# The RWKV-7 scan of a two-layer kernel without block-diagonal tiles

## The chip, the cores and the metric

The kernel runs on one core of a Trainium2 chip, as one program. The metric is the device time of one execution in microseconds (us). The time before is the median of 3 runs. The engines are named as in the profile: PE is TensorE's matrix products and PEld its weight loads, DVE is VectorE, ACT is ScalarE, POOL is GpSimd, SP is SyncE, which issues most of the DMAs.

## The reference

The program computes a hybrid block of two layers at width 1024 over 256 context and 1024 latent tokens, 1280 in all. The even layer mixes tokens by an mLSTM and an RWKV-7 head group, the odd one by HGRN2 and a latent attention. Each layer has a modulation and an MLP. The change concerns one piece of the even layer, the RWKV-7 recurrence, with 8 heads of 64 channels and two directions (the second runs over the flipped tokens):

```python
def rwkv7_scan(r, w, k, v, a_vec, b_vec):
    Z, T, H, dk = k.shape
    dv = v.shape[-1]
    xs = tuple(jnp.moveaxis(t, 1, 0) for t in (r, w, k, v, a_vec, b_vec))

    def step(S, inp):
        rt, wt, kt, vt, at, bt = inp
        sa = jnp.einsum('zhvk,zhk->zhv', S, at)
        S = S * wt[:, :, None, :] + sa[..., None] * bt[:, :, None, :] + vt[..., None] * kt[:, :, None, :]
        return S, jnp.einsum('zhvk,zhk->zhv', S, rt)

    _, y = lax.scan(step, jnp.zeros((Z, H, dv, dk), jnp.float32), xs)
    return jnp.moveaxis(y, 0, 1)
...
    y = rwkv7_scan(z(r), z(decay[0], decay[1]), z(key_d[0], key_d[1]), z(v), z(-kk), z(icl[0], icl[1]))
    y = head_groupnorm(dir_merge(y, B, n_ctx), rw_ln_w, rw_ln_b) + bonus
```

For each token the state S (64x64 a head) is decayed by w, corrected by the product of S with a and b, and given the outer product of v and k. The output is S times r. The two directions are added and normalized by head.

## The kernel before

**Tiling.** Tokens lie in 10 tiles of 128 (NT). The scan is computed in chunks of 64 tokens, two (cc) in a tile, so a direction has 20 chunk visits and both have 40. Within a chunk the recurrence is a triangular system: with u for the vector of all S·a of the chunk, u is the inverse of a triangular 64x64 matrix times a right-hand side that depends on the state at the chunk's start. The stage before (its products L854 to L936 are seen in rows of the prediction) computes these inverses, one for each head and chunk, and writes them to DRAM (xcd). Heads come in four pairs f; head e of a pair (0 or 1) lies on partitions 64e to 64e+63.

**The scan stage.** scan(d), L1001 to L1143, is a Python generator for direction d. L1278 weaves four generators with each other, a piece of each in turn: the gates of the mLSTM, scan(1), scan(0) and, at a rate of 0.6, the modulation's products (L245, with weights adaw that stream from HBM by DMA on SP's queue). From this order, and from priorities, a scheduler of the framework makes the order of instructions on each engine when the kernel is built; each engine then works through its own list and waits on semaphores. In this stage PSUM's eight banks are tagged (L986): three "ch" for the products of the ring, three "am" for the products that prepare a tile, one "mo" for the modulation, and one "ps" that only the gates use, at the start.

For each tile, load (L1004) issues the DMAs on SP's queue:

- CM holds the factors a and r with decay worked in, BK those of b and k (both from DRAM, by the stage before).
- ZV holds, for each chunk and head of a pair, the state on one partition half and v on the other. Later u takes the place of the state.
- XB[d][i], two buffers for each direction, holds the inverses of the pairs as block-diagonal 128x128 matrices. The off-diagonal blocks are set to zero once (L996, L997), and two DMAs a tile, one for each partition half, put the 64x64 inverses into the diagonal blocks (L1017).

amat (L1022) then prepares the tile in three parts: the products of BK with CM for each chunk (L1034), masked by VectorE into CM (L1037) and copied by ScalarE into AM (L1040 to L1042) for GpSimd to mask (L1044), and the turned BK (L1046 to L1056), which ScalarE copies into KB. These parts are done a tile ahead, between the chunk visits.

**One chunk visit** goes as follows (4 pairs f, the two heads e of a pair as two products each):

1. L1086, L1087: right-hand side pr, from CM and ZV (128 rows by 64 columns). L1089: VectorE copies it to rs.
2. L1094: pu = inverse times rs. The stationary operand is a column half of the block-diagonal XB, so 128 rows are read, of which 64 are zeros. Both heads go into one bank, on two partition halves. L1096: VectorE copies rows 0 to 63 of u into ZV; L1097: ScalarE copies rows 64 to 127.
3. L1105, L1106: pz, from KB and ZV. L1108: VectorE adds the state Zc to give t1. L1111, L1112: VectorE multiplies t1 by the chunk's decay (wlast) into ZV of the next chunk, half by half. L1114: GpSimd makes the next Zc from the same. L1116, L1117: ScalarE copies the new state from ZV into the block-diagonal ZB[d][i], whose other blocks are zeros (L996, L997, and L1070).
4. L1125, L1127: the output py. For each f come first two products of ZB (a column half, 128 rows) with r in CM, then two of u and v in ZV with AM, added to the same place in PSUM. L1134: ScalarE copies the output to yt, in the direction that reaches a tile first; in the other VectorE adds the first one's output, loaded back from DRAM (L1137).

A chunk's ring is 1, 2 and 3: the next right-hand side needs the state of L1111 and L1112. Step 4 is needed by nothing in the ring but stands in TensorE's list. After the second direction has done a tile, finish (L1145 to L1165) normalizes it and writes it out. The mLSTM stage follows, from about 1081 us of the span.

Of the kernel before, what the change touches and what calls it, by code (L numbers as in the profile page):

```python
# [17 lines left out]
P = 128  # L18
# [137 lines left out]
def _body(tc, nc, I, out, dbg, stop, es):  # L156
# [827 lines left out]
    with ExitStack() as ph:  # L984
# [6 lines left out]
        yfd = dram([NT, P, 4, P], "yfd")  # L991
        hfd = dram([NT, P, 512], "hfd")

        XB = [[rp.tile([P, 2, 4, P], F32, name=f"XB{d}{i}") for i in range(2)] for d in range(2)]
        ZB = [[rp.tile([P, 4, P], F32, name=f"ZB{d}{i}") for i in range(2)] for d in range(2)]
        for t_ in XB[0] + XB[1] + ZB[0] + ZB[1]:  # L996
            G.memset(t_, 0.0)  # L997
        lnb_eps = rp.tile([P, 1], F32, name="lneps")
        V.memset(lnb_eps, RW_GN_EPS)

        def scan(d):  # L1001
            bst4 = strict.unsqueeze(1).to_broadcast((P, 4, 64))

            def load(step):  # L1004
                c = ORD[d][step]
                xb = XB[d][step % 2]
                CM = rp.tile([P, 4, 3, P], F32, tag="CM", name=nm("CM"), bufs=4)
                BK = rp.tile([P, 4, 2, 2, 64], F32, tag="BK", name=nm("BK"), bufs=3)
                ZV = rp.tile([P, 2, 2, 4, 64], F32, tag="ZV", name=nm("ZV"), bufs=4)
                SY.dma_start(CM[0:64, :, 0:2, :], ard[d][c, 0:64])  # L1010
                SY.dma_start(CM[64:128, :, 1:3, :], ard[d][c, 64:128])
                SY.dma_start(BK, bkd[d][c])
                for e in range(2):
                    q = slice(64 * e, 64 * e + 64)
                    SY.dma_start(ZV[64 - 64 * e:128 - 64 * e, :, e].rearrange("p c f v -> p c (f v)"),
                                 vtd[d][c * P:(c + 1) * P, e].rearrange("(c t) f v -> t c (f v)", c=2))
                    SY.dma_start(xb[q, :, :, 64 * e:64 * e + 64].rearrange("p c f t -> p (c f) t"),  # L1017
                                 xcd[d, q, 2 * c:2 * c + 2].rearrange("p c f t -> p (c f) t"))
                return dict(c=c, xb=xb, CM=CM, BK=BK, ZV=ZV)

            def amat(o):
# [38 lines left out]
            for part in amat(cur):  # L1060
                part()
                yield
            zi = 0
            for cc_ in (0,):
                G.memset(cur["ZV"][0:64, 0, 0], 0.0)
                G.memset(cur["ZV"][64:128, 0, 1], 0.0)
            Zc = rp.tile([P, 4, 64], F32, tag=f"Zc{d}", name=nm("Zc"), bufs=2)
            G.memset(Zc, 0.0)
            for i in range(2):
                G.memset(ZB[d][i], 0.0)  # L1070
            for step in range(NT):
                nxt, parts = None, []
                if step + 1 < NT:
# [5 lines left out]
                for cc in range(2):  # L1079
                    tk = slice(64 * cc, 64 * cc + 64)  # L1080
                    last = step == NT - 1 and cc == 1
                    uv, zb = ZV[:, cc], ZB[d][zi % 2]
                    pr = ps(256, tag="ch")
                    for f in range(4):
                        o = pr[:, f * 64:f * 64 + 64]
# [2 lines left out]
                    rs = rp.tile([P, 4, 64], F32, tag="rs", name=nm("rs"), bufs=2)  # L1088
                    V.tensor_copy(rs, pr.rearrange("p (f v) -> p f v", f=4))  # L1089
                    yield  # L1090
                    pu = ps(256, tag="ch")
                    for f in range(4):
                        for e in (0, 64):
                            TE.matmul(pu[e:e + 64, f * 64:f * 64 + 64], xb[:, cc, f, e:e + 64], rs[:, f, :], start=True, stop=True)  # L1094
                    puv = pu.rearrange("p (f v) -> p f v", f=4)
                    V.tensor_copy(uv[0:64, 0], puv[0:64])  # L1096
                    S.copy(uv[64:128, 1], puv[64:128])  # L1097
                    if parts:
                        parts.pop(0)()
                    yield  # L1100
                    if not last:
                        pz = ps(256, tag="ch")
                        for f in range(4):
                            o = pz[:, f * 64:f * 64 + 64]
                            TE.matmul(o[0:64], KB[:, 0, cc, f, :], uv[:, 0, f, :], start=True, stop=True)  # L1105
                            TE.matmul(o[64:128], KB[:, 1, cc, f, :], uv[:, 1, f, :], start=True, stop=True)  # L1106
                        t1 = rp.tile([P, 4, 64], F32, tag="t1", name=nm("t1"), bufs=2)
                        V.tensor_tensor(t1, pz.rearrange("p (f v) -> p f v", f=4), Zc, op=ALU.add)  # L1108
                        wb = wlast[:, d, :, 2 * c + (cc if d == 0 else 1 - cc)].unsqueeze(2).to_broadcast((P, 4, 64))
                        zn = ZV[:, 1] if cc == 0 else nxt["ZV"][:, 0]  # L1110
                        V.tensor_tensor(zn[0:64, 0], t1[0:64], wb[0:64], op=ALU.mult)  # L1111
                        V.tensor_tensor(zn[64:128, 1], t1[64:128], wb[64:128], op=ALU.mult)  # L1112
                        Zc = rp.tile([P, 4, 64], F32, tag=f"Zc{d}", name=nm("Zc"), bufs=2)
                        G.tensor_tensor(Zc, t1, wb, op=ALU.mult)  # L1114
                        zbn = ZB[d][(zi + 1) % 2]
                        S.copy(zbn[0:64, :, 0:64], zn[0:64, 0])  # L1116
                        S.copy(zbn[64:128, :, 64:128], zn[64:128, 1])  # L1117
                    if parts and cc:
                        parts.pop(0)()
                    yield  # L1120
# [1 line left out]
                    for f in range(4):  # L1122
                        o = py[:, f * 64:f * 64 + 64]
                        for e in (0, 64):
                            TE.matmul(o[e:e + 64], zb[:, f, e:e + 64], CM[:, f, 1, tk], start=True, stop=False)  # L1125
                        for e in range(2):
                            TE.matmul(o[64 * e:64 * e + 64], uv[:, e, f, :], AM[:, cc, e, f, :], start=False, stop=True)  # L1127
                    zi += 1
                    pyv = py.rearrange("p (f t) -> p f t", f=4)
                    if cc == 0 and not first:  # L1130
                        yo = rp.tile([P, 4, P], F32, tag=f"yo{d}", name=nm("yo"), bufs=1)
# [885 lines left out]
```

## Time and profile before

| | |
|---|---|
| time, median of 3 runs | 4004.09 us (3995.06 to 4010.38) |
| the profiled execution's own time | 3995.29 us |
| its span, first to last instruction | 3993.5 us |
| TensorE's granted clock over the span (1 is full speed) | 0.952 |
| the stage before the scan, its last 50 us (715 to 765 us): TensorE busy, clock | 39.3 us, 0.85 |
| the scan stage (765 to 1081 us): its length | 316 us |
| the mLSTM stage, its first 79 us (1081 to 1160 us): TensorE busy, clock | 57.6 us, 0.87 |
| the scan's output products, L1125 and L1127: TensorE busy | 44.9 and 44.6 us |
| the u products, L1094 | 29.8 us |

The profile is of one execution, and its own time stands 9 us below the median of the runs. In the rows of the profile, a group such as "L1125 PE MATMUL ps<-CM,ZB 128*64 128x64 f32 x640" names the line, the engine, the operation, the tile written and those read, and the tile form: "128*64" means that 128 rows and 64 columns of the array are used; "128x64" is the moving operand, and x640 the count. Two products whose forms leave room for each other (two column halves, or two row halves) run side by side. Behind the shape stand the busy time in us and the mean duration of one in ns, then the idle time of the engine before them and what ended it. "<-issue" means that nothing that the profile shows was waited for. A row of a timeline has the start in us from the span's start, the length, the engine and the group; [0.47 <-X] is idle time ahead of it that X ended.

### The profile page before, as it was taken

To read this page: it belongs to the slowest core of one execution; us is meant where nothing else is said; L and a number is where in the kernel's file an instruction comes from. 1 tells how busy PE (TensorE), PEld (TensorE's weight loads), DVE (VectorE), ACT (ScalarE), POOL (GpSimd) and SP (SyncE) were. 2 spreads that over 40 slices of the span, in tenths; PEclk is the share of its full clock that TensorE was granted. 3 is DMA by queue.
4 is the path that set the end of the run, shared out by engine and by line. 5 is a ranking of instruction groups with operands and counts; after the bars stand their busy time and mean duration, and the time that the engine had idled before them with its cause. 6 is when DMAs were issued, how large, how long until landed. Compare 5 with 4: busy or idle time off the path is not lost. (4 is left out here: it accounts for less than half of the span.)

```text
span 3993.5 us, 67013 instructions
## 1 busy us (share of the span) xinstructions
PE 3634.5 (91%) x26934; PEld 3113.5 (78%) x26934; DVE 2308.7 (58%) x3891; ACT 1346.4 (34%) x2569; POOL 1493.1 (37%) x1532
## 2 busy tenths in 40 slices
PE   5999989888788799999999989988888979999998
PEld 3888879766577698998999878976666758888887
DVE  5565553355557656556656632338878466666655
ACT  3444342354533432214222232223344434223221
POOL 3044646433333443324332221334444535333332
PEclk7999999899889899999999999989999989999999
DMA  4454646779577632223222276222122364334332
GB/s 168 124 135 126 164 117 160 190 215 230 178 259 260 202 91 86 80 75 116 80 80 69 83 223 194 92 100 73 59 81 72 108 198 127 100 101 137 95 100 74
DMA packets 534911, 521.33 MB, mean 131 GB/s; under 512 B 128296, under 2 KB 443624, under 8 KB 534600
## 3 DMA queue, kind: packets, MB, share of 16 engines
q1 hardware_dynamic: 438904, 441.03, 37.7%
q10 hardware_dynamic: 82080, 35.17, 3.1%
q0 software_dynamic: 13616, 40.84, 2.9%
q8 instruction: 212, 3.47, 0.4%
q14 instruction: 99, 0.81, 0.1%
HBM read 395.79 MB, written 121.16 MB: 129 GB/s over the span
## 5 line engine op out<-in xcount | busy, mean ns | idle before, releaser
L281 ACT CAST wh<-raw 128x1024 fp32r<-128x1024 f32 x330 | 341.2, 1050 | 1000.5 <-PE ps L288 502.1
L286 PE MATMUL ps<-mh,wh 128*128 128x384 f32 (+2 forms) x1888 | 630.5, 334 | 4.5 <-ACT mh L337 3.0
L288 PE MATMUL ps<-mh,wl 128*128 128x256 f32 (+2 forms) x1888 | 626.8, 332 | 4.4 <-POOL wl L282 4.4
L287 PE MATMUL ps<-mh,wh 128*128 128x256 f32 (+2 forms) x1888 | 626.8, 332 | 0.0
L471 DVE TENSOR_TENSOR relu<-relu 128x384 f32<-128x384 f32 (+1 forms) x192 | 332.7, 1733 | 396.7 <-ACT relu L470 396.6
L282 POOL TENSOR_TENSOR wl<-raw,wh 128x1024 fp32r<-128x1024 f32 x145 | 351.6, 2425 | 538.7 <-ACT wh L281 537.1
L286 PE MATMUL ps<-wh,h1h 128*128 128x512 f32 x1152 | 450.5, 391 | 5.1 <-ACT acc L502 2.7
L287 PE MATMUL ps<-wl,h1h 128*128 128x512 f32 x1152 | 449.3, 390 | 0.0
L288 PE MATMUL ps<-wh,h1l 128*128 128x512 f32 x1152 | 449.3, 390 | 0.0
L504 DVE TENSOR_TENSOR acc<-ps,acc 128x512 f32<-128x512 f32 x540 | 359.2, 684 | 153.3 <-PE ps L288 150.7
L473 POOL TENSOR_TENSOR h1l<-relu,h1h 128x384 fp32r<-128x384 f32 (+1 forms) x192 | 202.5, 1055 | 531.6 <-DVE h1h L472 527.4
L286 PEld LDWEIGHTS ps<-mh,wh 128*128 128x128 f32 x1888 | 357.8, 190 | 38.9 <-issue 11.1
L288 PEld LDWEIGHTS ps<-mh,wl 128*128 128x128 f32 x1888 | 357.5, 189 | 24.9 <-POOL wl L282 4.8
L287 PEld LDWEIGHTS ps<-mh,wh 128*128 128x128 f32 x1888 | 357.7, 189 | 21.7 <-POOL mh L338 0.3
L282 DVE TENSOR_TENSOR wl<-raw,wh 128x1024 fp32r<-128x1024 f32 x185 | 236.3, 1300 | 212.9 <-ACT wh L281 206.1
L288 PE MATMUL ps<-hh,wl 128*128 128x256 f32 (+2 forms) x992 | 316.4, 319 | 14.6 <-DVE wl L282 14.6
L286 PE MATMUL ps<-hh,wh 128*128 128x256 f32 (+2 forms) x992 | 325.1, 328 | 3.7 <-DVE hh L639 3.7
L287 PE MATMUL ps<-hl,wh 128*128 128x256 f32 (+2 forms) x992 | 318.8, 321 | 5.1 <-POOL hl L640 4.5
L286 PEld LDWEIGHTS ps<-wh,h1h 128*128 128x128 f32 x1152 | 216.7, 188 | 50.2 <-ACT acc L502 3.4
L288 PEld LDWEIGHTS ps<-wh,h1l 128*128 128x128 f32 x1152 | 216.8, 188 | 45.3
L287 PEld LDWEIGHTS ps<-wl,h1h 128*128 128x128 f32 x1152 | 216.9, 188 | 43.4 <-DVE wl L282 0.2
L288 PEld LDWEIGHTS ps<-hh,wl 128*128 128x128 f32 x992 | 194.3, 196 | 15.8 <-DVE wl L282 15.3
(534 smaller groups left out, 7327.8 us busy)
## 6 DMA issues: line engine op xcount, KB each, us to landing
raw<-in_mlp_w SPq DMA_DIRECT2D x256, 512.0 KB, 4.0
adaw<-in_ada_w SPq DMA_DIRECT2D x96, 512.0 KB, 5.0
raw<-in_ev_w SPq DMA_DIRECT2D x46, 512.0 KB, 3.9
bkd<-BK SPq DMA_DIRECT2D x16, 640.0 KB
CM<-ard SPq DMA_DIRECT2D x40, 256.0 KB, 8.8
BK<-bkd SPq DMA_DIRECT2D x20, 512.0 KB, 6.0
qk<-qkd SPq DMA_DIRECT2D x20, 512.0 KB, 8.3
fk<-fkd SPq DMA_DIRECT2D x20, 512.0 KB, 5.2
```

Source lines behind the costliest of these rows:

```text
L281: S.copy(h, raw)
L282: (leng or G).tensor_tensor(l, raw, h, op=ALU.subtract)
L286: TE.matmul(o, lh, rh, start=first, stop=False)
L287: TE.matmul(o, lh, rl, start=False, stop=False)
L288: TE.matmul(o, ll, rh, start=False, stop=last)
L471: V.tensor_tensor(r_, r_, r_, op=ALU.mult)
L473: G.tensor_tensor(l_[:, t0:t1], r_, a[:, t0:t1], op=ALU.subtract)
L504: V.tensor_tensor(acc[i][:, cs_], pt, acc[i][:, cs_], op=ALU.add)
```

## The change

It concerns the scan stage alone. The tiles XB and ZB go, and with them the memsets of L997 and L1070 and ScalarE's copies L1116 and L1117. The inverses are loaded into a tile xb of half the size, as they are stored in DRAM (both heads' 64x64 blocks on their own partition halves), by one DMA a tile instead of two. The u product reads 64 rows for each head, on the head's row half, and puts the two heads into two PSUM banks: the first into a "ch" bank, the second into the "ps" bank. VectorE and ScalarE each read their own bank. The output product with the state reads the 64 rows of a head from Zc, which holds the state without block-diagonal form. The products with AM (L1127) stay as they were.

```diff
@@ -991,10 +991,6 @@
         yfd = dram([NT, P, 4, P], "yfd")
         hfd = dram([NT, P, 512], "hfd")
 
-        XB = [[rp.tile([P, 2, 4, P], F32, name=f"XB{d}{i}") for i in range(2)] for d in range(2)]
-        ZB = [[rp.tile([P, 4, P], F32, name=f"ZB{d}{i}") for i in range(2)] for d in range(2)]
-        for t_ in XB[0] + XB[1] + ZB[0] + ZB[1]:
-            G.memset(t_, 0.0)
         lnb_eps = rp.tile([P, 1], F32, name="lneps")
         V.memset(lnb_eps, RW_GN_EPS)
 
@@ -1003,7 +999,7 @@
 
             def load(step):
                 c = ORD[d][step]
-                xb = XB[d][step % 2]
+                xb = rp.tile([P, 2, 4, 64], F32, tag=f"xb{d}", name=nm("xb"), bufs=2)
                 CM = rp.tile([P, 4, 3, P], F32, tag="CM", name=nm("CM"), bufs=4)
                 BK = rp.tile([P, 4, 2, 2, 64], F32, tag="BK", name=nm("BK"), bufs=3)
                 ZV = rp.tile([P, 2, 2, 4, 64], F32, tag="ZV", name=nm("ZV"), bufs=4)
@@ -1011,11 +1007,9 @@
                 SY.dma_start(CM[64:128, :, 1:3, :], ard[d][c, 64:128])
                 SY.dma_start(BK, bkd[d][c])
                 for e in range(2):
-                    q = slice(64 * e, 64 * e + 64)
                     SY.dma_start(ZV[64 - 64 * e:128 - 64 * e, :, e].rearrange("p c f v -> p c (f v)"),
                                  vtd[d][c * P:(c + 1) * P, e].rearrange("(c t) f v -> t c (f v)", c=2))
-                    SY.dma_start(xb[q, :, :, 64 * e:64 * e + 64].rearrange("p c f t -> p (c f) t"),
-                                 xcd[d, q, 2 * c:2 * c + 2].rearrange("p c f t -> p (c f) t"))
+                SY.dma_start(xb.rearrange("p c f t -> p (c f t)"), xcd[d, :, 2 * c:2 * c + 2].rearrange("p c f t -> p (c f t)"))
                 return dict(c=c, xb=xb, CM=CM, BK=BK, ZV=ZV)
 
             def amat(o):
@@ -1060,14 +1054,11 @@
             for part in amat(cur):
                 part()
                 yield
-            zi = 0
             for cc_ in (0,):
                 G.memset(cur["ZV"][0:64, 0, 0], 0.0)
                 G.memset(cur["ZV"][64:128, 0, 1], 0.0)
             Zc = rp.tile([P, 4, 64], F32, tag=f"Zc{d}", name=nm("Zc"), bufs=2)
             G.memset(Zc, 0.0)
-            for i in range(2):
-                G.memset(ZB[d][i], 0.0)
             for step in range(NT):
                 nxt, parts = None, []
                 if step + 1 < NT:
@@ -1079,7 +1070,7 @@
                 for cc in range(2):
                     tk = slice(64 * cc, 64 * cc + 64)
                     last = step == NT - 1 and cc == 1
-                    uv, zb = ZV[:, cc], ZB[d][zi % 2]
+                    uv, zb = ZV[:, cc], Zc
                     pr = ps(256, tag="ch")
                     for f in range(4):
                         o = pr[:, f * 64:f * 64 + 64]
@@ -1088,13 +1079,14 @@
                     rs = rp.tile([P, 4, 64], F32, tag="rs", name=nm("rs"), bufs=2)
                     V.tensor_copy(rs, pr.rearrange("p (f v) -> p f v", f=4))
                     yield
-                    pu = ps(256, tag="ch")
+
+                    pus = [ps(256, tag=t_).rearrange("p (f v) -> p f v", f=4) for t_ in ("ch", "ps")]
                     for f in range(4):
-                        for e in (0, 64):
-                            TE.matmul(pu[e:e + 64, f * 64:f * 64 + 64], xb[:, cc, f, e:e + 64], rs[:, f, :], start=True, stop=True)
-                    puv = pu.rearrange("p (f v) -> p f v", f=4)
-                    V.tensor_copy(uv[0:64, 0], puv[0:64])
-                    S.copy(uv[64:128, 1], puv[64:128])
+                        for e, pu in enumerate(pus):
+                            q = slice(64 * e, 64 * e + 64)
+                            TE.matmul(pu[q, f], xb[q, cc, f, :], rs[q, f, :], start=True, stop=True)
+                    V.tensor_copy(uv[0:64, 0], pus[0][0:64])
+                    S.copy(uv[64:128, 1], pus[1][64:128])
                     if parts:
                         parts.pop(0)()
                     yield
@@ -1112,9 +1104,6 @@
                         V.tensor_tensor(zn[64:128, 1], t1[64:128], wb[64:128], op=ALU.mult)
                         Zc = rp.tile([P, 4, 64], F32, tag=f"Zc{d}", name=nm("Zc"), bufs=2)
                         G.tensor_tensor(Zc, t1, wb, op=ALU.mult)
-                        zbn = ZB[d][(zi + 1) % 2]
-                        S.copy(zbn[0:64, :, 0:64], zn[0:64, 0])
-                        S.copy(zbn[64:128, :, 64:128], zn[64:128, 1])
                     if parts and cc:
                         parts.pop(0)()
                     yield
@@ -1122,10 +1111,9 @@
                     for f in range(4):
                         o = py[:, f * 64:f * 64 + 64]
                         for e in (0, 64):
-                            TE.matmul(o[e:e + 64], zb[:, f, e:e + 64], CM[:, f, 1, tk], start=True, stop=False)
+                            TE.matmul(o[e:e + 64], zb[e:e + 64, f, :], CM[e:e + 64, f, 1, tk], start=True, stop=False)
                         for e in range(2):
                             TE.matmul(o[64 * e:64 * e + 64], uv[:, e, f, :], AM[:, cc, e, f, :], start=False, stop=True)
-                    zi += 1
                     pyv = py.rearrange("p (f t) -> p f t", f=4)
                     if cc == 0 and not first:
                         yo = rp.tile([P, 4, P], F32, tag=f"yo{d}", name=nm("yo"), bufs=1)
```

## The prediction

> **What bounds the kernel now.** I read the page first, for the span. Its shares are averages over stages with other limits, and the change touches only the RWKV scan, so I went on to that stage.
>
> ```profile
> span 3993.5 us, 67013 instructions
> ```
>
> The groups by line put the scan's products between about 765 and 1081 us. The sums of that window say what is full there (columns: length, busy time and count of each engine, clock, DMA share, GB/s):
>
> ```profile
> 765.00:1081.00 316.00, 264.23 (x4523) 208.89 (x4520) 167.96 (x368) 167.43 (x356) 112.67 (x112) 0.91 0.80 212
> ```
>
> TensorE 264 of 316 us, VectorE and ScalarE 168 each, GpSimd 113. The waits of this stage (who <- for whom: us in total, times, longest) show the direction:
>
> ```profile
> DVE rs L1089 <- PE ps L1087: 27.1, 18, 5.4
> ...
> PEld ps L1125 <- issue: 7.3, 5, 2.4
> ...
> PE ps L1127 <- issue: 5.6, 3, 2.3
> ...
> PEld ps L245 <- DMA adaw<-in_ada_w: 4.2, 4, 1.5
> PEld ps L1094 <- ACT ZV L1097: 4.1, 4, 1.2
> ...
> PEld ps L1105 <- ACT ZV L1097: 3.5, 3, 1.2
> ...
> PEld ps L1106 <- ACT ZV L1097: 2.9, 8, 0.8
> ...
> PEld ps L1087 <- DVE ZV L1112: 1.0, 2, 0.5
> ```
>
> VectorE waits for TensorE (27.1 us for the right-hand side alone). The place that decides is the step from one chunk to the next: the right-hand side (L1086, L1087) needs the state from VectorE (L1111, L1112), yet TensorE waits for L1112 only 1.0 us in all. Between the state product (L1105, L1106) and the next right-hand side, TensorE's own queue (the output products L1125 and L1127, the modulation products L245, the next tile's L1034) is therefore longer than VectorE's path. So the ring runs through every instruction in TensorE's queue, and whatever is added at L1125 adds to the stage nearly one for one.
>
> **The change part by part.**
>
> *The output product on row halves (L1125).* The group (busy us, mean ns | idle before) gives the count:
>
> ```profile
> L1125 PE MATMUL ps<-CM,ZB 128*64 128x64 f32 x640 | 44.9, 233 | 3.8 <-issue 1.9 <-DVE t L1108 1.6 <-DVE yt L1137 0.3
> ```
>
> 640 over 40 chunk visits: 16 a visit, in four groups of four (one for each f), each followed by four of L1127. Both are 128 rows by 64 columns today; afterwards L1125 is 64*64 and L1127 stays 128*64. The timeline of two visits shows the price of a group today:
>
> ```profile
> 895.51 0.34 PE L1125 MATMUL ps<-CM,ZB 128*64 128x64 f32 x4
> 895.67 0.29 PE L1127 MATMUL ps<-AM,ZV 128*64 128x64 f32 x4
> 895.79 0.29 PE L1125 MATMUL ps<-CM,ZB 128*64 128x64 f32 x4
> 895.91 0.29 PE L1127 MATMUL ps<-AM,ZV 128*64 128x64 f32 x4
> 896.02 0.29 PE L1125 MATMUL ps<-CM,ZB 128*64 128x64 f32 x4
> ```
>
> From 895.67 to 896.02 are three groups: 0.117 us a group, 0.058 a pair, and 0.94 for the eight of a visit. L1125 and L1127 follow one another at no cost while their forms are equal. What does another form cost? Three places, each from its own stretch of the timeline:
>
> ```profile
> 154.33 1.26 PE L936 MATMUL ps<-AR,BK 64*64 64x64 f32 x36 [0.47 <-DVE Wp L873]
> 155.53 0.41 PE L286 MATMUL ps<-hh,wh 128*128 128x322 f32 x1
> ```
> ```profile
> 132.96 0.31 PE L287 MATMUL ps<-hl,wh 128*128 128x322 f32 x1
> 133.10 0.30 PE L288 MATMUL ps<-hh,wl 128*128 128x322 f32 x1
> 133.34 0.54 PE L854 MATMUL ps<-al,lr 64*128 64x320 f32 x2
> ```
> ```profile
> 862.10 0.27 PE L1086 MATMUL ps<-ZV,CM 128*64 128x64 f32 x1
> 862.10 0.27 PE L1087 MATMUL ps<-ZV,CM 128*64 128x64 f32 x1
> 862.20 0.22 PE L1086 MATMUL ps<-ZV,CM 128*64 128x64 f32 x1
> 862.21 0.22 PE L1087 MATMUL ps<-ZV,CM 128*64 128x64 f32 x1
> 862.26 0.28 PE L1086 MATMUL ps<-ZV,CM 128*64 128x64 f32 x2
> ```
>
> L936 is the very form that L1125 gets: two row halves side by side. Its 36 take 1.26 us; less the last one's own 0.22 (a product of 64 columns lasts that long in the other rows too) that is 1.04 over 35 steps, 0.059 us a pair, as fast as 128*64. So the halves themselves neither gain nor lose. But L936's last start is 155.37, and the next form starts at 155.53: 0.16 instead of 0.06. From L287 to L288 it is 0.14 from start to start, from L288 to the row halves of L854 0.24, again 0.10 more, and there the rows alone change. After a change the second pair also comes late: L1086 follows another form (64*128) at 862.10, and its pairs start at 862.10, 862.20 and 862.26, 0.10 and then 0.06; in the first group above, behind L245, 895.51 to 895.67 is 0.16 where the next ones take 0.117. Together a change of form costs 0.10 + 0.05 = 0.15 us. A visit gets eight (into and out of 64*64 for each f), 320 in all, less some 7 where another form already stands ahead: 313 x 0.15 = **+47 us**. The trace has no 64*64 next to 128*64, so the bounds are 0 (only some pairs of forms pay) and 47; I take 47, since all three places pay, whether rows, columns or both change.
>
> [...]
>
> *The u product on row halves (L1094).* Two more changes of form a run of it, into and out; about half of these runs already stand beside L245, another form, and a change ahead of a wait for rs is hidden. Between 0 and 40 x 2 x 0.15 = 12 us: I take **+4**.
>
> *u through two banks.* Today ScalarE's copy starts only when VectorE's, from the same bank, has ended:
>
> ```profile
> 1000.71 0.42 DVE L1096 COPY ZV<-ps 64x256 f32<-64x256 f32 x1 [0.86 <-PE ps L1094]
> 1001.22 0.37 ACT L1097 COPY ZV<-ps 64x256 f32<-64x256 f32 x1 [2.30 <-DVE ZV L1096]
> 1001.63 0.55 PEld L1094 LDWEIGHTS ps<-rs,XB 128*64 128x64 f32 x16 [1.18 <-ACT ZV L1097]
> ```
>
> With a bank each they start together, 0.51 us earlier for ScalarE. It counts where TensorE waits for that copy: 4 + 3 + 8 = 15 times (waits above), **-7 us**; the bound is 40 x 0.51 = -20. Against it: the second bank is the only one of its kind and both directions use it, so where both u products now run back to back the second must wait for ScalarE's copy of the first, about 1.18 - 0.51 = 0.67 us. What is queued behind that wait is the state product, which would have waited for the same copy; I count 0, bound +0.67 x 10 = +7.
>
> *The copies into ZB and the memsets go.*
>
> ```profile
> L1116 ACT COPY ZB<-ZV 64x256 f32<-64x256 f32 x38 | 15.4, 406 | 27.0 <-DVE ZV L1111 26.5
> L1117 ACT COPY ZB<-ZV 64x256 f32<-64x256 f32 x38 | 15.3, 403 | 15.4 <-DVE ZV L1112 14.5 <-DMA grd<-mrow 0.7
> ```
> ```profile
> L997 POOL MEMSET XB<- 128x1024 f32 x4 | 3.6, 941 | 0.0
> ```
>
> 31 us of ScalarE go, but those copies run while TensorE does L1125 and L1127, and no row has anyone waiting for L1116 or L1117. Behind them in ScalarE's queue stand yt copies, wanted a chunk later: 0, bound -0.4 x 20 = -8. L1125 then reads Zc, which GpSimd writes a chunk ahead: no new wait. GpSimd's memsets (3.6 us for XB, about as much for ZB) run ahead of the scan's first loads, under the previous stage's products: -1.
>
> *One load of the inverses instead of two.*
>
> ```profile
> XB<-xcd SPq DMA_DIRECT2D x40, 128.0 KB, 7.9
> ```
>
> Twenty issues go, and rows of 2 KB replace pieces of 256 B. No product waits for XB's landing (L1094 waits for rs and ZV alone), so it is hidden: -1, for the modulation weights behind it on SP's queue.
>
> *What absorbs.* The stalls marked "issue" at L1125 and L1127, 7.3 + 5.6 = 12.9 us, end at times that TensorE's pace need not move, and 4.2 us wait for weights by DMA. A later TensorE meets them later. Bounds 0 and -17; I take about half, **-9**.
>
> Sum: 47 + 4 - 7 - 1 - 1 - 9 = **+33 us**. The profiled execution took 3995.29 us (its span 3993.5, so 1.8 lie around it); the median shown is 4004.09, 9 above. The difference goes on the median: **4037 us**.
>
> **The rivals.**
>
> *Not slower: 64*64 and 128*64 need no change.* If a form of 64 columns could pass to another one freely, L1125 and L1127 would follow one another as they do now. Against it: L854, where the rows alone change, pays too; but at 128 columns, so no row quite excludes this. Then the u banks (-7), loads and memsets (-2) and some of ScalarE's 8 us are left: 4004 - 9 to -20, 3984 to 3995. It decides from a price below about 0.03 us a change (9 us over 313).
>
> *Hidden: TensorE has more room than its queue shows.* The stalls absorb all 17 us and the u copies give their full 20: 47 + 4 - 17 - 20 - 2 = +12, 4016 us. For it: VectorE, ScalarE and TensorE wait for each other all through the stage. Against it: the 1.0 us at L1112.
>
> *Slower still: the clock.* The granted clock of the stage is 0.91 on the whole, and lower at its start:
>
> ```profile
> 765.00:800.00 35.00, 32.78 (x525) 28.35 (x522) 16.84 (x37) 18.14 (x45) 13.22 (x13) 0.78 1.10 278
> ```
>
> A group of four would take 0.117 + 0.15 = 0.27 us for the same streaming, so the array streams 44% of that time. Should the stage's clock fall from 0.91 to 0.82, TensorE's 264 us grow by a tenth, 26 us: 4063. [...]
>
> **How the numbers follow.** Forecast (4018 to 4058) 0.55; hidden (3996 to 4018) 0.18; no price (3975 to 3996) 0.14; clock (4058 to 4085) 0.13. The range 3988 to 4068 leaves out about half of each outer case, 0.15 together. A measurement of this kernel tells about 0.5%, 20 us, from no change (3984 to 4024). Faster: not quite half of the no-price case, 0.06. Same: its rest 0.08, the hidden case 0.18 and the forecast's lower edge 0.06, 0.32. Slower: 0.49 + 0.13 = 0.62.
>
> **What would show it.** In the changed profile: L1125 as 64*64; groups of L1125 and L1127 some 0.27 us apart, a visit 2.1 us instead of 0.94; L1097 starting with L1096 and TensorE's waits for it near 0.7 us; no L1116, L1117; the scan some 33 us longer and the stages beside it unmoved. Groups still 0.117 us apart make me wrong at once; groups at 0.27 with a scan of the old length mean that the ring did not run through TensorE's queue. The order of instructions on the engines is made anew when the kernel is built and may shift the stage by some us either way, which no row can tell.

## The result and the profile after

The changed kernel takes 4033.52 us (median of 5 runs, 4014.15 to 4046.19), the kernel before 4007.56 us in the same comparison. The ratio is 1.0073, with a 95% interval from 1.0046 to 1.0100, so the change makes the kernel 0.7% slower, about 29 us. The forecast was 4037 us. The number was right, but only in part for the reasons given: two of its small terms were wrong by 31 and 23 us with opposite signs, and that they nearly cancel is luck.

Lines have moved: the right-hand side is now L1077 and L1078 (before L1086, L1087), the u product L1087 (L1094), VectorE's and ScalarE's copies of u L1088 and L1089 (L1096, L1097), the state product L1097 and L1098, the output product with the state L1114 (L1125) and that with AM L1116 (L1127).

The scan's first product (L1034, now L1028) starts at 763.4 us in the profile before and at 753.6 after, its last output product ends at 1080.7 and 1103.3: the stage is 32 us longer. The profile after is of the shortest of the five executions, 4014.15 us, so its whole span is only 19 us longer than that of the profile before. The sums of the stage after (length; busy us and count of TensorE, its loads, VectorE, ScalarE, GpSimd; clock, DMA share, GB/s):

```profile
754.00:1104.00 350.00, 325.41 (x4547) 241.79 (x4544) 175.02 (x375) 135.81 (x283) 111.10 (x112) 0.92 0.67 192
```

TensorE is busy for 93% of the stage, where it was 84%, and ScalarE has lost the 31 us of the copies into ZB. The groups of the lines that changed (busy us, mean ns | idle before):

```profile
L1114 PE MATMUL ps<-CM,Zc 64*64 64x64 f32 x640 | 58.0, 250 | 0.7 <-DVE yt L1125 0.7
L1116 PE MATMUL ps<-AM,ZV 128*64 128x64 f32 x640 | 57.3, 254 | 0.0
...
L1087 PE MATMUL ps<-rs,xb 64*64 64x64 f32 x640 | 40.6, 238 | 12.5 <-ACT ZV L1089 6.9 <-DVE rs L1080 5.2
...
L1089 ACT COPY ZV<-ps 64x256 f32<-64x256 f32 x40 | 14.7, 368 | 67.7 <-PE ps L1087 66.7 <-DMA ZV<-vtd 0.8
```

Both output groups have grown, from 45 to 58 and 57 us, though L1116 was not touched, and the u product from 29.8 to 40.6. L1116 no longer waits for anything ("issue" was 5.6 us there). ScalarE's copy of u now waits for TensorE (66.7 of its 67.7 us) and no longer for VectorE, as meant. But the products of L1087 wait 6.9 us for that copy, and their weight loads 9.0:

```profile
PEld ps L1087 <- ACT ZV L1089: 9.0, 11, 3.1
```

Before, the loads waited 4.1 us for it there and 6.4 at the state product (3.5 and 2.9). Behind the change the state product no longer waits for ScalarE's copy: the gain that was forecast came, and a longer wait at the next u product took it back. The timeline of one stretch of output products shows the price that was forecast:

```profile
875.46 0.33 PE L1114 MATMUL ps<-CM,Zc 64*64 64x64 f32 x4
875.72 0.34 PE L1116 MATMUL ps<-AM,ZV 128*64 128x64 f32 x4
875.98 0.33 PE L1114 MATMUL ps<-CM,Zc 64*64 64x64 f32 x4
876.24 0.34 PE L1116 MATMUL ps<-AM,ZV 128*64 128x64 f32 x4
876.51 0.33 PE L1114 MATMUL ps<-CM,Zc 64*64 64x64 f32 x4
```

From 875.46 to 876.51 are four groups, 0.262 us each, against 0.117 before: 0.145 us for a change of form, where 0.15 was forecast.

### The profile page after: what moved, and what is told of

Same layout as the page of the kernel before. It is cut to its first block, busy times and chain, and to the rows that moved or that the text cites. A ratio compares the mean times of both kernels' runs of the same rounds, so it can differ in the third digit from the quotient of the medians.

```text
span 4012.4 us, 66916 instructions
## 1 busy us (share of the span) xinstructions
PE 3684.1 (92%) x26934; PEld 3136.4 (78%) x26934; DVE 2316.2 (58%) x3891; ACT 1313.5 (33%) x2491; POOL 1486.4 (37%) x1520
```

## The experiments

All times are in the table below; the ratio is to the kernel before, run beside each. "Rows" means products on row halves (64 rows a head), "stored" means inverses loaded as stored by one DMA.

| run | output product with the state | u product | inverses | banks for u | median us | ratio (95% interval) |
|---|---|---|---|---|---|---|
| before | 128 rows | 128 rows | block-diagonal | one | 4000 to 4008 | 1 |
| after | rows | rows | stored | two | 4033.52 | 1.0073 (1.0046 to 1.0100) |
| e1_out_block | 128 rows | rows | stored | two | 3992.33 | 0.9987 (0.9975 to 0.9999) |
| e2_out_alone | rows | 128 rows | block-diagonal | one | 4044.11 | 1.0116 (1.0102 to 1.0130) |
| e3_banks_alone | 128 rows | 128 rows | block-diagonal | two | 4002.85 | 1.0005 (0.9991 to 1.0020) |
| e4_regroup | rows, regrouped | rows | stored | two | 3998.33 | 1.0001 (0.9992 to 1.0009) |
| e5_regroup_xb | rows, regrouped | 128 rows | block-diagonal | one | 4000.03 | 1.0003 (0.9990 to 1.0017) |
| e6_u_one_bank | rows | rows | stored | one | 4004.98 | 1.0013 (1.0000 to 1.0026) |
| e7_regroup_one_bank | rows, regrouped | rows | stored | one | 3973.83 | 0.9938 (0.9918 to 0.9958) |
| e8_u_rows_alone | 128 rows | rows | block-diagonal | one | 3997.43 | 0.9991 (0.9981 to 1.0002) |
| e9_u_stored | 128 rows | rows | stored | one | 3978.35 | 0.9939 (0.9921 to 0.9956) |
| e10_u_pieces | 128 rows | rows | two loads in 256-byte pieces, no memset | one | 4002.89 | 0.9998 (0.9986 to 1.0011) |
| e11_four_ch | rows | rows | stored | two of four | 4006.95 | 1.0015 (1.0000 to 1.0031) |
| e12_one_load_pieces | 128 rows | rows | one load in 256-byte pieces | one | 3983.73 | 0.9954 (0.9935 to 0.9974) |

### The output product: undone, alone, and in another order

e1_out_block is the changed kernel with ZB, its copies and the old output product back:

```diff
-    TE.matmul(o[e:e + 64], zb[e:e + 64, f, :], CM[e:e + 64, f, 1, tk], start=True, stop=False)
+    TE.matmul(o[e:e + 64], zb[:, f, e:e + 64], CM[:, f, 1, tk], start=True, stop=False)
...
+    S.copy(zbn[0:64, :, 0:64], zn[0:64, 0])
+    S.copy(zbn[64:128, :, 64:128], zn[64:128, 1])
```

> The change with the output product (L1125 of before) read from block-diagonal copies again, on 128 rows; ScalarE's copies and two memsets are back, everything else is as after. Theory (the changes of form at the output product cost the time): some 300 changes go, at 0.145 us each 45 us of TensorE, of which about 10 to 20 come back as waits, so 4033 becomes about 4005 (3995 to 4015), and the step from one group of four to the next is 0.117 us again. Rival (the u product on row halves with its second bank is what costs): within 8 us of the changed kernel, about 4030.

It came to 3992 us: the theory holds, and by more than expected; without the new output product the change would have been 5 us faster than before. e2_out_alone is the reverse: that edit alone in the kernel before.

> The kernel before with the output product alone on row halves, from Zc, without ZB and its copies; the inverses, their loads and the u product are as before. Theory: groups 0.262 us apart, +45 us of TensorE, less 10 to 17 us of absorbed waits: 4007 becomes about 4038 (4030 to 4050). Rival (u costs): within 8 us of the kernel before.

4044 us, +46: this edit alone costs more than the whole change. In its profile, L1125 is L1118 and L1127 is L1120:

```profile
L1120 PE MATMUL ps<-AM,ZV 128*64 128x64 f32 x640 | 59.4, 261 | 0.0
L1118 PE MATMUL ps<-CM,Zc 64*64 64x64 f32 x640 | 56.9, 258 | 6.1 <-DVE t L1104 2.8 <-issue 2.5 <-DVE yt L1129 0.6
```

In this pair of kernels TensorE's list of instructions in the scan is the same but for the operands, as it is between e1_out_block and the changed kernel. So the 46 us come from the edit and not from another order; most other pairs differ in this list as well (below). The sums of the stage, from its first product to its last, before and in e2_out_alone:

```profile
763.00:1081.00 318.00, 266.14 (x4535) 210.79 (x4536) 168.69 (x373) 168.39 (x359) 112.67 (x112) 0.90 0.81 212
```
```profile
764.00:1124.00 360.00, 319.38 (x4535) 240.61 (x4536) 171.52 (x372) 138.04 (x283) 110.81 (x112) 0.87 0.71 187
```

TensorE is busy for 53 us more, and its idle time falls from 52 to 41: 11 us were absorbed. The granted clock is lower too, 0.87 instead of 0.90 in the stage, and 0.946 to 0.948 over the span in all four executions, where the median of the kernel before beside it is 0.952. At 0.87 the stage's 360 us lose 47 to the clock, at 0.90 its 318 lose 32; so, as an estimate, up to 15 of the 53 us can be the clock's. Why it is lower was not tried.

e4_regroup keeps the row halves and changes only the order, so that a visit changes form twice and not eight times:

```diff
     for f in range(4):
         o = py[:, f * 64:f * 64 + 64]
         for e in (0, 64):
-            TE.matmul(o[e:e + 64], zb[e:e + 64, f, :], CM[e:e + 64, f, 1, tk], start=True, stop=False)
+            TE.matmul(o[e:e + 64], zb[e:e + 64, f, :], CM[e:e + 64, f, 1, tk], start=f == 0, stop=False)
+    for f in range(4):
+        o = py[:, f * 64:f * 64 + 64]
         for e in range(2):
-            TE.matmul(o[64 * e:64 * e + 64], uv[:, e, f, :], AM[:, cc, e, f, :], start=False, stop=True)
+            TE.matmul(o[64 * e:64 * e + 64], uv[:, e, f, :], AM[:, cc, e, f, :], start=False, stop=f == 3)
```

> The change with the output product in another order: all four pairs' products with the state first, then all four with AM, so a visit changes its form twice instead of eight times. The first product of a bank's half alone starts the accumulation. Theory: 240 changes go, 240 x 0.145 = 35 us of TensorE, 10 to 15 us of it come back as waits: 4033 becomes about 4010 (4000 to 4018). Rival (the time is the row halves themselves, or u, not the changes of form): within 8 us of the changed kernel.

3998 us: the changes of form cost the time, not the row halves. The regrouping gives back 0.7%, about 29 us, of the 35 worked out, a little more than expected. TensorE's list also shifts elsewhere in this pair. In e5_regroup_xb below, against e2_out_alone, the regrouping gives back 44. Four accumulations are now open in a bank at once, and only the first product of each half is marked with a start; what a start for each of them would do was not run.

### Two banks for u

e3_banks_alone splits u over two banks in the kernel before, its products still on 128 rows:

```diff
-    pu = ps(256, tag="ch")
+    pus = [ps(256, tag=t_).rearrange("p (f v) -> p f v", f=4) for t_ in ("ch", "ps")]
```

> The kernel before with u alone through two banks; all products stay on 128 rows, so no change of form is added. Theory of the prediction: ScalarE's copy starts with VectorE's, 7 us faster (bound 20), about 4000. Rival: the one second bank is shared by both directions, so the second u product waits for ScalarE's copy of the first and its halves run one behind the other: 5 to 15 us slower than before, 4012 to 4022.

4003 us, +0.05%, with an interval that reaches from -0.1 to +0.2%: neither the forecast gain of 7 us nor the rival's loss, of which only the lower edge fits. e6_u_one_bank answers for the changed kernel itself: u goes back into one bank, still on row halves.

```diff
-    pus = [ps(256, tag=t_).rearrange("p (f v) -> p f v", f=4) for t_ in ("ch", "ps")]
+    pu = ps(256, tag="ch").rearrange("p (f v) -> p f v", f=4)
...
-    S.copy(uv[64:128, 1], pus[1][64:128])
+    S.copy(uv[64:128, 1], pu[64:128])
```

> The change with both halves of u in one 'ch' bank as before, on row halves, inverses as stored. Theory (the shared second bank costs): the halves run side by side again (in the change some 110 of 320 pairs did not, 6 us), and the three waits of a u product for ScalarE's copy of the other direction's (7.6 us) go, while ScalarE's copy starts behind VectorE's again: 10 us faster to 5 slower than the changed kernel, 4023 to 4038. Rival (the two banks gain 7 to 20 us, as the prediction had it): 4040 to 4050.

4005 us: 0.60% below the changed kernel, 24 us, more than the theory expected. Two banks cost here. The timeline of the changed kernel shows two ways. First, two u products of the two directions follow each other:

```profile
835.25 0.68 PE L1087 MATMUL ps<-rs,xb 64*64 64x64 f32 x16
...
836.41 0.68 PE L1087 MATMUL ps<-rs,xb 64*64 64x64 f32 x8
...
839.79 0.37 ACT L1089 COPY ZV<-ps 64x256 f32<-64x256 f32 x1
...
840.58 0.54 PEld L1087 LDWEIGHTS ps<-rs,xb 64*64 64x64 f32 x8 [0.41 <-ACT ZV L1089]
840.58 0.67 PE L1087 MATMUL ps<-rs,xb 64*64 64x64 f32 x8
```

The first direction's 16 products take 0.68 us, both heads side by side. The second direction's first head (8 products, "ch" bank) takes 0.68 us alone, and its second head comes only at 840.58, when ScalarE has emptied the single "ps" bank, and takes 0.67 again. Of the 640 u products, 182 start within 25 ns of the one before in the changed kernel, 310 in e6_u_one_bank. The 128 pairs that came apart take 0.058 us more each: 7 us. Second, where the order has nothing else to do, TensorE stands still:

```profile
1003.40 0.33 PE L1087 MATMUL ps<-rs,xb 64*64 64x64 f32 x2 [1.47 <-DVE rs L1080]
...
1004.30 1.28 ACT L1147 ACT_TABLE_LOAD   x1
...
1005.60 0.63 ACT L1147 ACTIVATE fq<-fq 128x512 f32<-128x512 f32 x1
1006.25 0.37 ACT L1089 COPY ZV<-ps 64x256 f32<-64x256 f32 x1
...
1006.67 1.01 PE L1087 MATMUL ps<-rs,xb 64*64 64x64 f32 x14 [2.95 <-ACT ZV L1089]
```

ScalarE is at the norm of a finished tile (L1147, with a table load of 1.28 us ahead of it), so the copy that frees the bank starts at 1006.25, and the other direction's u product stands for 2.95 us; the 6.9 us above are three such places. e7_regroup_one_bank takes the second bank away from the regrouped kernel:

> The regrouped output product (3998 with two banks for u) with both halves of u in one bank, on row halves, inverses as stored. Theory (the shared second bank costs): 3988 to 3998. Rival (two banks gain): 4003 to 4015.

3974 us, below what either theory gave, and 0.63% below e4_regroup: 25 us again. It is 0.6% faster than the kernel before. Do two banks cost, or does it cost that both directions share the only second one? e11_four_ch gives the gates' bank to the "ch" group, and both halves of u take theirs from four:

```diff
-    sb.enter_context(psum(ch=3, am=3, ps=1, mo=1))
+    sb.enter_context(psum(ch=4, am=3, mo=1))
...
-    pus = [ps(256, tag=t_).rearrange("p (f v) -> p f v", f=4) for t_ in ("ch", "ps")]
+    pus = [ps(256, tag="ch").rearrange("p (f v) -> p f v", f=4) for _ in range(2)]
```

> The changed kernel with both u banks taken in turn from four 'ch' banks; the bank that was kept for the gates is the fourth, and the gates use 'ch' too. Theory (what costs 24 us in the change is that the second bank is one and shared by both directions): 4000 to 4015, as with u in one bank (4005). Rival (two banks for u as such separate the halves and cost): 4025 to 4040, as the changed kernel.

4007 us, as with one bank. The split is there and its cost is gone: 283 of the u products start close behind another, and those that wait for ScalarE's copy wait 1.7 us instead of 6.9. So in this kernel the sharing of one bank by two directions costs, and not the split. TensorE's list differs between these kernels too, which no run here takes apart; and in the kernel before the same shared bank (e3_banks_alone) costs next to nothing.

### The inverses as stored

e5_regroup_xb is the regrouped output product with u as before the change (block-diagonal inverses, one bank).

> The output product on row halves in the order of the run before (two changes of form a visit), and u as in the kernel before: block-diagonal inverses, one bank, two loads. With eight changes this pairing took 4044 (the output product alone on row halves). Theory: 240 changes fewer, -35 us of TensorE, and since TensorE waits more than it did there (43.5 us of stalls over 0.45 us), 0 to 14 of them come back: 4010 to 4022, no better than the kernel before, whose 640 products had no change at all. Rival (ScalarE's copies and the ZB traffic were worth something): 3985 to 4000.

4000 us, the upper edge of what the rival expected. It stands 26 us above e7_regroup_one_bank, which differs in nothing but the u product's rows and the tile and load of the inverses. Of these, e8_u_rows_alone makes the first in the kernel before, without the second:

```diff
-    TE.matmul(pu[e:e + 64, f * 64:f * 64 + 64], xb[:, cc, f, e:e + 64], rs[:, f, :], start=True, stop=True)
+    TE.matmul(pu[e:e + 64, f * 64:f * 64 + 64], xb[e:e + 64, cc, f, e:e + 64], rs[e:e + 64, f, :], start=True, stop=True)
```

> The kernel before with the u product alone on row halves: it reads the diagonal blocks of the block-diagonal inverses, 64 rows each; one bank, loads and memsets as before. Theory: two changes of form a run of u products, 80 x 0.15 = 12 us of TensorE at most, part of it in waits: 4000 becomes 4000 to 4010. Rival (the order that the builder makes with row halves in u is what took 33 us of stalls to 25 in the changed kernel): 3985 to 3996.

3997 us, -0.09%: nothing that can be told from no change. e9_u_stored makes both:

> The kernel before with the inverses as stored, one load a tile, and u on row halves in one bank; the output product stays on 128 rows with its copies. The runs so far differ by this part alone in two pairs: 4044 against 4005 with eight changes of form in the output, 4000 against 3974 with two. Theory (the part is worth 26 to 40 us by itself, beside -3.6 for the row halves without it): 3962 to 3978. Rival (it only gives back what the row halves of the output cost, because both then share a form): 3990 to 4004.

3978 us, -0.6%, 24 us. This part of the change, alone, gains. e10_u_pieces asks which piece of it: the tile is taken in turn and no longer set to zero, the two loads stay.

```diff
-                xb = XB[d][step % 2]
+                xb = rp.tile([P, 2, 4, P], F32, tag=f"xb{d}", name=nm("xb"), bufs=2)
```

> As the run with u alone on row halves from the diagonal blocks, but the tile of the inverses is no longer set to zero and takes turns as the other tiles do; the two loads in pieces of 256 bytes stay. Theory 1 (the single load in rows of 2 KB is what gains): as with the row halves alone, 3992 to 4002. Theory 2 (the memset and the fixed tiles held the loads up): as with the inverses as stored, 3962 to 3980.

4003 us: not the memsets or the fixed tiles. e12_one_load_pieces has one load, but with the small pieces:

```diff
-    SY.dma_start(xb.rearrange("p c f t -> p (c f t)"), xcd[d, :, 2 * c:2 * c + 2].rearrange("p c f t -> p (c f t)"))
+    SY.dma_start(xb[:, :, :, 0:64].rearrange("p c f t -> p (c f) t"), xcd[d, :, 2 * c:2 * c + 2].rearrange("p c f t -> p (c f) t"))
```

> As the run with the inverses as stored and the output product unchanged (3978), but its one load a tile writes into a tile with gaps, so it moves the same pieces of 256 bytes as before the change. The built list of TensorE is nearly that of the 3978 run, while with two loads (in pieces or in rows of 2 KB) it is nearly that of the 4003 run. Theory (the order of the work that the builder makes with one load gains, not the size of the pieces): 3970 to 3988. Rival (the pieces take the DMA engines' time and cost): 3994 to 4006.

3984 us, -0.46%: most of the gain, 19 of 24 us, stays with pieces of 256 bytes. One sentence of this expectation doesn't hold: this kernel's list for TensorE is a third one. Place by place, half of it holds the same kind of product as that of e9_u_stored, and two thirds as that of the kernel before.

The gain goes with a change of the list. In the scan TensorE's list is the same in before, e2, e8 and e10, and before, e8 and e10 take the same time. In e9_u_stored only 38% of the places hold the same kind of product as in before. What that does can be seen between the two kernels e10_u_pieces and e9_u_stored, in TensorE's waits of the stage for the copy of u and for t1 (u product, state product, output product are L1093, L1104 and L1105, L1124 in the first; u and state product L1092, L1102, L1103 in the second). First e10_u_pieces:

```profile
PEld ps L1093 <- ACT ZV L1096: 4.1, 4, 1.2
...
PEld ps L1105 <- ACT ZV L1096: 3.6, 8, 1.2
PEld ps L1104 <- ACT ZV L1096: 3.5, 3, 1.2
...
PEld ps L1104 <- DVE t L1107: 2.5, 3, 1.1
...
PEld ps L1124 <- DVE t L1107: 2.4, 3, 1.1
```

and e9_u_stored:

```profile
PEld ps L1103 <- ACT ZV L1094: 3.5, 2, 3.1
...
PEld ps L1092 <- ACT ZV L1094: 1.3, 4, 0.5
...
PEld ps L1102 <- DVE t L1105: 0.8, 1, 0.8
...
PEld ps L1102 <- ACT ZV L1094: 0.6, 3, 0.3
```

These rows come to 16 us in the first and 6 in the second. In e10_u_pieces both directions stand at the same step with no other work between them:

```profile
992.88 0.37 ACT L1096 COPY ZV<-ps 64x256 f32<-64x256 f32 x1 [2.30 <-DVE ZV L1095]
...
993.30 0.68 PE L1093 MATMUL ps<-rs,xb 64*64 64x64 f32 x16 [1.04 <-ACT ZV L1096]
...
994.60 0.37 ACT L1096 COPY ZV<-ps 64x256 f32<-64x256 f32 x1 [1.35 <-DVE ZV L1095]
...
995.02 0.27 PE L1104 MATMUL ps<-ZV,KB 128*64 128x64 f32 x1 [1.04 <-ACT ZV L1096]
```

In e9_u_stored the next tile's products stand between such steps more often, in portions. Part of one tile's, with the ring's steps between them (left out here):

```profile
921.36 1.16 PE L1031 MATMUL ps<-CM,BK 64*128 64x128 f32 x8
...
924.46 1.16 PE L1031 MATMUL ps<-CM,BK 64*128 64x128 f32 x8
...
926.59 1.16 PE L1031 MATMUL ps<-CM,BK 64*128 64x128 f32 x8
...
928.85 1.16 PE L1031 MATMUL ps<-CM,BK 64*128 64x128 f32 x16
```

where e10_u_pieces has 48 in one piece, ten times in the stage (e9_u_stored has three such pieces):

```profile
932.38 4.46 PE L1033 MATMUL ps<-CM,BK 64*128 64x128 f32 x48
```

The sums of the stage agree: TensorE does the same work in a stage 16 us shorter (e10_u_pieces from its first product to its last, then e9_u_stored):

```profile
758.00:1072.00 314.00, 264.68 (x4528) 209.76 (x4530) 168.02 (x371) 168.38 (x359) 112.73 (x112) 0.92 0.81 214
```
```profile
761.00:1059.00 298.00, 260.99 (x4534) 201.63 (x4534) 174.01 (x371) 167.87 (x359) 112.16 (x112) 0.95 0.76 225
```

TensorE's idle time makes 12 of the 16 us (49 to 37) and its busy time 4. The clock is 0.95 instead of 0.92, and what share of the 16 it has can't be told. These two executions, 3991 and 3983 us, also lie closer together than the medians.

So the form of the load changes the order of the work, and the gain shows mainly as waits that other work now covers. That the order is the cause, and not the one DMA issue fewer, is argued from the waits. It was not tried apart: a kernel with the two loads and e9_u_stored's order was not made. One run speaks against the portions as the whole reason: e12_one_load_pieces gains 19 us and still has eight of its pieces of 48 whole.

## Why the number was right and two of its terms were not

From before to after there is a path of neighbours, each of which differs from the last in one part (in us at 4000 us, from the ratios; each is uncertain by 4 to 12 us to either side). The total comes out because +31 us at the bank and -23 at the load nearly cancel.

| step | from, to | forecast | measured |
|---|---|---|---|
| u product on row halves | before, e8 | +4 | -4 |
| no XB tiles and memsets | e8, e10 | -1 (with ZB's) | +3 |
| inverses as stored, one load | e10, e9 | -1 | -24 |
| output product on row halves, no ZB copies | e9, e6 | +47, and -9 absorbed | +30 |
| second bank for u | e6, after | -7 | +24 |
| together | | +33 | +29 |

**What bounds the stage** held. The ring runs through TensorE's list: where the list is the same and only the form changes (before against e2), the stage grows by 42 us for 53 of TensorE's busy time.

**The price of a change of form** held: 0.145 us (0.262 less 0.117 us a group) against 0.15, between 64*64 and 128*64, which no row of before had. That answers the first rival (no price between these forms). That the time is in the change and not in the row halves is shown by the order alone: two changes a visit instead of eight give 29 us back (after against e4).

**Absorption** was put at -9, between 0 and -17. TensorE's idle time in the stage bears it out: with this edit it falls by 11 us (before to e2, 52 to 41), 8 (e1 to after, 33 to 25) and 17 (e9 to e6, 37 to 20). The lists of each pair are the same, those of the third but for some places; the time grows by 46, 34 and 30 us. The way to the -9 had an error, though. The 7.3 us are a row of the weight loads and the 5.6 a row of the products, and the longest stalls stand in both: that up to 908.00 us is 2.35 us ahead of a load of L1125 and 2.27 ahead of a product of L1127. Their sum of 12.9 counts these twice; the products' own rows of L1125 and L1127 give 1.9 + 5.6 = 7.5. The second rival (most of it hidden, +12 in all) is ruled out by the total, whose interval is 18 to 40 us, and by the 30 to 46 that the output product costs by itself.

**The u product and the memsets** held within the measurement: neither can be told from nothing. The ZB copies were not taken out by themselves: they go in every kernel whose output product is on row halves, so what they were worth is contained in its 30 to 46 us.

**Two banks for u** is the first step that failed. The prediction saw the other side ("the second bank is the only one of its kind and both directions use it") and put it at 0, with a bound of +7, because the state product behind it would have waited anyway. Two things were missed: the halves of u come apart and no longer run side by side (7 us), and the copy that frees the bank stands in ScalarE's list behind a tile's norm, so that the wait is up to 2.95 us and not 0.67 (6.9 us). In e6_u_one_bank the state product waits 3.0 us for ScalarE's copy, which the changed kernel doesn't, so the second makes 4 us more, and both make 11 of the 24. The rest is not settled: TensorE's list is another one as well, with 38% of the places alike. Nor is the share of the 7: in e3_banks_alone the halves come apart too (149 of 640 start close behind another, 283 in before), yet the split costs 2 us there, not 24.

**One load instead of two** is the second: "hidden: -1". It asked only who waits for this DMA, and the answer was right: nobody. But the load's form goes into the order in which the kernel is built, and the change of load is worth 24 us. That it is by the order is argued, not shown. The prediction's last paragraph named this as what no row can tell, "some us either way"; it was the largest gain in the change.

**The third rival (the clock)** came in part. In the profile after the stage has 0.92, where the row of before has 0.91, so the 26 us did not come there. But the same edit goes with 0.87 instead of 0.90 in e2_out_alone, and with 0.92 instead of 0.95 from e9 to e6; only from e1 to after is it 0.92 in both. The five times of the changed kernel follow the clock of their spans, from 4014 us at 0.956 to 4046 at 0.947. What lowers it is not shown.

The stages beside the scan were unmoved within what one execution tells. The scan began 10 us earlier in the profile after, but TensorE's last product of the stage ahead of it (L684), which no kernel here changes, ended at 745.6 us in before, at 740.1 us in after, and anywhere from 738.6 us (e1) to 750.0 us (e7) in the others.

The version to keep is e9_u_stored or e7_regroup_one_bank, 0.6% faster than before: the inverses as stored with u in one bank, and the output product either block-diagonal as before or on row halves in the regrouped order.

## What to carry to other kernels

Small products of unlike tile form should be grouped by form where a change costs what it did here, between 64*64 and 128*64: with 58 ns a pair, one change of 0.145 us cost as much as two and a half pairs, and a change in every group of four took the group from 0.117 to 0.262 us. A bank of which there is only one can tie together two chains that are meant to fill each other's gaps: here that cost 24 us in one order of the work (e6 to after) and 2 us, no more than the measurement tells from nothing, in another (e3). Look in the list of the engine that frees it for what stands ahead. And where a scheduler makes the order of the work, an edit that no engine waits for can still move the time by half a per cent, so the parts of a change have to be timed apart before one of them is kept or dropped. A price in TensorE's time is best checked as two sums of the stage, busy and idle, with the granted clock beside them.

## What the runs showed of the hardware that was not expected

In the kernel before, TensorE's long waits marked "issue" stand beside packets of a DMA queue that the profile calls "instruction". TensorE's weight loads have seven such waits of over 1 us (1.02 to 2.35) between 781 and 1081 us. Each begins 0.6 to 1.7 us after the start of a 16-KB packet of that queue; 34 of these packets start in that time, and each takes 0.9 to 1.7 us. The longest wait, 2.35 us up to 908.00, begins 0.6 us after the packet of 905.07. Of seven shorter waits, of 0.76 to 0.93 us, one begins 1.8 us after the start of such a packet, the other six 4.5 us after one or later. In e10_u_pieces five of the six waits of over 1 us begin 0.7 to 1.9 us after a packet; in the profile after there is only one, of 1.27 us, and no packet starts within 5 us ahead of it. That the packets are TensorE's program, and that the waits are for it, is the author's inference: in each 400 us of the span of before there is one packet for 244 to 264 instructions of PE and PEld. This was seen in traces and not tried by a run.
